# A decoder layer on one core: the two gate rows of the modulation as column sums on VectorE, a DRAM row and a broadcast load, in place of TensorE's sum over partitions

## The chip, the cores and the metric

One core of one Trainium2 chip runs the whole layer in one launch. The metric is the device time in microseconds (us). Before the change it is 745.29 us, the median of 3 runs (744.9 to 745.97).

## The reference, cut to what matters

The kernel computes one decoder layer for T = 512 tokens of width D = 1024: a token-mixing half with two attention branches (16 heads in all, one input projection) and a channel half with a gated MLP of 2 x 2816 hidden columns and a causal convolution of width 3 over the tokens. Each half is scaled, shifted and gated by six rows that come from one conditioning vector c:

```python
mod = c @ w_ada + b_ada
sh1, sc1, gt1, sh2, sc2, gt2 = [m[:, None, :] for m in jnp.split(mod, N_MOD, axis=-1)]
u = x * (1.0 + sc1) + sh1
...
x = _layer_norm(DEEPNORM_ALPHA * x + (1.0 + gt1) * attn_out, ln1_g, ln1_b)
u2 = x * (1.0 + sc2) + sh2
...
x = _layer_norm(DEEPNORM_ALPHA * x + (1.0 + gt2) * ffn_out, ln2_g, ln2_b)
```

The change concerns the two gates, `gt1` and `gt2`, called gate1 and gate2 below, alone. Each is a vector of 1024 numbers that multiplies along the columns of a weight (w_o and w_down), so the kernel needs it as a row repeated on all 128 partitions; shift and scale multiply along the rows of the transposed activations, so they are needed as columns (128 partitions x 8).

## The kernel before, in words

**Stages.** The profile's span falls into these stretches: start, until the first matmul of the input projection at 9.98 us; the first columns of the input projection, k step by k step (L307, to about 50 us); the attention, where heads are interleaved with the rest of the projections (to about 300 us); output projection and first LayerNorm (to about 395 us); the MLP (L1126, 44 steps n, to about 665 us); and the last products with the second LayerNorm (to 743 us). The large matmuls are float32 split into a high and a low part (`wh`, `wl`, made by ScalarE at L183 and VectorE at L93), three products each (L134, L135, L136). The down projection of the MLP is done in a Strassen form, on sums and differences of blocks of w_down, which VectorE makes (L953 to L979).

**Weights.** SyncE issues the loads (L157) in program order into five rotating raw buffers of 128 x 1024; a buffer is loaded again when its last reader is done. For some tiles of w_down, GpSimd issues a second DMA that adds another block onto the loaded tile (L162). The items are taken in one list; the 32 modulation tiles `wa1` are among them.

**Order.** A scheduler with a cost model sets the order of the instructions on TensorE (PE), VectorE (DVE), ScalarE (ACT) and GpSimd (POOL) from the program; only SyncE stays as written. Each engine then runs its list in order, and a wait of one instruction holds all that stand behind it.

**The modulation.** At the start, `mod_sum` (L201) makes shift1 and scale1 as columns: a tile of the transposed w_ada (128 outputs x 1024 inputs) is multiplied on DVE by `cbc`, which is c repeated on all partitions, and summed along the row (`accum_out`). L244 adds 1 to the bias columns of the two scales, and L247 makes the columns `modc` from which ACT makes the first operand `uh` (L273). The later 16 tiles for shift2 and scale2 go the same way (L583).

For the gates, `ada_proc` (L580) takes another layout: four tiles for each half row of 512 outputs, eight blocks of 128 inputs x 512 outputs, which DVE multiplies by a column of c (`cTs`) and adds up (L588 once, L593 seven times). The sum over the 128 partitions is left: `ada_split` (L597) makes the high and low part `ach` and `acl`, and `ada_sum` (L606) multiplies both by a 128 x 128 matrix of ones on PE (L612, L613), so that every partition gets the sum; DVE adds it and 1 (L615) to the bias, which SyncE loaded broadcast over the partitions (L574, 512 KB). There are four half rows: both of gate1 in the attention, the high half of gate2 at n = 10 and 11 of the MLP (L1140, L1142), the low half at n = 28 and 30.

**Who uses them.** gate1 (`gt` of index 0) multiplies the tiles of w_o at L640, from 270.1 us on. gate2 multiplies blocks of w_down: its high half first at L953, at 474.18 us, in a chain L953, L954, L955, L958 and two splits `wdl` (L93) that PE waits for at L1104.

Of the kernel before, what the change touches and what calls it, by code (L numbers as in the profile page):

```python
# [16 lines left out]
P = 128  # L17
T = 512
D = 1024
KT = D // P  # L20
# [28 lines left out]


@with_exitstack
def layer_kernel(ctx: ExitStack, tc: tile.TileContext, out, xT, x, cT, crow, wa0, wa1, bcol, bgt, w1, wct, wv, bf,
                 wp, wo, lncol, lnrow, wup, cwb, wdp):
    nc = tc.nc
    ctx.enter_context(tc.manual_schedule(engines={nc.sync.engine}))
# [3 lines left out]
    t13 = [tc.dram_tile([P, 1024], F32, name=f"t13_{p}") for p in range(FP)]  # L59
    wgt = [tc.dram_tile([P, 512], F32, name=f"wgt_{q}") for q in range(FP)]  # L60
    t24 = tc.dram_tile([P, 1024], F32, name="t24")
    st1 = ExitStack()
    stg = ctx.enter_context(tc.tile_pool(name="stg", bufs=1))
    pp = ctx.enter_context(tc.tile_pool(name="pp", bufs=8, space=PSUM))
# [11 lines left out]
    def bank():  # L76
        return pp.tile([P, 512], F32, name=nm("ps"), tag="ps")
# [5 lines left out]
    def const(shape, dt, s):  # L83
        return cons.tile(shape, dt, name=s, tag=s)
# [4 lines left out]
    def hi_of(o, i, scale=1.0):  # L89
        S.activation(o, i, AF.Copy, scale=scale)  # L90

    def lo_of(o, i, hi):
        state["read"] = V.tensor_tensor(o, i, fl(hi), ALU.subtract)  # L93
        return state["read"]
# [23 lines left out]
    V.tensor_copy(identb, ident)  # L118
    zerob = preset([P, P], BF16, "zerob")
# [8 lines left out]
    modr = const([P, 4, KT, 2], F32, "modr")  # L128

    def z(dt, s, shape=(P, 512)):  # L130
        return zp.tile(list(shape), dt, name=nm(s), tag="z", bufs=NZ)
# [69 lines left out]
    def mod_sum(w, col, wt, c, e):  # L201
        o = modr[:, w, col, e : e + 1]
        state["read"] = V.scalar_tensor_tensor(wt[:, c], wt[:, c], 1.0, cbc[:, c], ALU.mult, ALU.mult, accum_out=o)
        return state["read"]
# [31 lines left out]
    def first_acc(j):  # L236
        wa = pend[j][0]
        if j == 0:
            for e in range(2):
                for q in range(2):  # L240
                    s = mod_sum(q, j, wa[q], slice(e * 512, (e + 1) * 512), e)
            with tc.issue_after(s.ins):
                for q in (1, 3):
                    V.tensor_scalar_add(bcols[:, q, :], bcols[:, q, :], 1.0)  # L244
            for q in range(2):
                raw = modr[:, q, j, :]
                state["modc"] = V.scalar_tensor_tensor(modc[:, q, j : j + 1], raw[:, 0:1], raw[:, 1:2], bcols[:, q, j : j + 1], ALU.add, ALU.add)  # L247
        else:
            mod_col(0, j, wa[0])
            state["modc"] = mod_col(1, j, wa[1])  # L250
# [318 lines left out]
            hi_of(yh[p], yf[p])  # L569
            lo_of(yl[p], yf[p], yh[p])  # L570

    def gt_tile(i):
        t = cons.tile([P, D], F32, name=f"gt{i}", tag="gt")
        nc.sync.dma_start(t, bgt[i : i + 1, :].broadcast_to([P, D]))  # L574
        return t

    gt = [None, None]
    ada_st = {}

    def ada_proc(n):  # L580
        def f(r):
            if 8 <= n < 24:
                mod_sum(2 + (n - 8) // 8, n % 8, r, slice(0, D), 0)  # L583
                return
            g, q = n // 4, n % 4
            if q == 0:
                ada_st[g] = z(F32, "ac2")
                V.tensor_scalar_mul(ada_st[g], r[:, 0:512], cTs[:, 0:1])  # L588
            acc = ada_st[g]
            for e in range(2):  # L590
                k = 2 * q + e
                if k > 0:
                    a = V.scalar_tensor_tensor(acc, r[:, e * 512 : (e + 1) * 512], cTs[:, k : k + 1], acc, ALU.mult, ALU.add)  # L593
                    state["read"] = a
        return f

    def ada_split(g, n):  # L597
        weights(n, 0)
        acc = ada_st[g]
        ah, al = z(F32R, "ach"), z(F32R, "acl")  # L600
        hi_of(ah, acc)
        lo_of(al, acc, ah)
        ada_st[g] = ah, al
        yield 0

    def ada_sum(g):  # L606
        ah, al = ada_st.pop(g)
        ps = bank()
        i = 0 if g < 2 else 1
        if gt[i] is None:  # L610
            gt[i] = gt_tile(i)
        PE.matmul(ps, onesr, ah, start=True, stop=False)  # L612
        PE.matmul(ps, onesr, al, start=False, stop=True)  # L613
# [55 lines left out]
    def add_ada(n=1):  # L669
        for _ in range(n):  # L670
            if skip[0]:
                skip[0] -= 1
            elif adas[0] < 24:
                add_item(wa1[adas[0]], ada_proc(adas[0]))
                adas[0] += 1
                if adas[0] in (4, 8):
                    stream.append((ada_split, (adas[0] // 4 - 1, len(items) - 1)))
                    sums.append([len(stream) + 3, adas[0] // 4 - 1])

    marks = {}  # L680
    seq = PAIRS
# [4 lines left out]

    def flush_sum(n):
        if sums and n >= sums[0][0]:
            stream.append((ada_sum, (sums.pop(0)[1],)))

    wpi = {}

# [612 lines left out]
def _pack(inputs):  # L1305
# [5 lines left out]
    wk = w_ada.reshape(KT, P, 6, D)  # L1311
    r = {}
    r["xT"] = c(a["x"][0].T)
    r["x"] = a["x"][0]
# [7 lines left out]
    r["bcol"] = c(bm[[0, 1, 3, 4]].transpose(2, 0, 1))  # L1322
    r["bgt"] = c(a["b_ada"].reshape(6, D)[[2, 5]])
    def col(kind, n):
        if kind in ("sb", "fox"):
            return (4104 if kind == "sb" else 3080) + n * P
# [23 lines left out]
    return r  # L1350


_NAMES = ["xT", "x", "cT", "crow", "wa0", "wa1", "bcol", "bgt", "w1", "wct", "wv", "bf", "wp", "wo", "lncol", "lnrow",
          "wup", "cwb", "wdp"]


# [17 lines left out]
```

## Time and profile before

| | |
|---|---|
| time, median of 3 runs | 745.29 us (744.9 to 745.97) |
| profiled execution, span | 743.3 us |
| its own time beside the span | the page gives the span alone; the median is 2.0 us above it |
| PE (TensorE matmul) busy | 732.6 us, 99% of the span, 3476 matmuls |
| DVE (VectorE) busy | 607.5 us, 82% |
| ACT (ScalarE) busy | 390.1 us, 52% |
| POOL (GpSimd) busy | 81.5 us, 11% |
| the chain that ended last | PE 98%, POOL 1%, DVE 1% |

A row of the profile names the line of the kernel, the engine, the operation, what is written and read, and how many there were, then the busy time and the mean duration in ns, then the idle time just ahead of them and what ended it. A row of the timeline begins with the start and the duration in us. Matmuls overlap: the duration of one is longer than the distance from its start to the next start, and the distance is what a matmul costs.

### The profile page before, as it was taken

To read this page: it belongs to the slowest core of one execution; us is meant where nothing else is said; L and a number is where in the kernel's file an instruction comes from. 1 tells how busy PE (TensorE), PEld (TensorE's weight loads), DVE (VectorE), ACT (ScalarE), POOL (GpSimd) and SP (SyncE) were. 2 spreads that over 40 slices of the span, in tenths; PEclk is the share of its full clock that TensorE was granted. 3 is DMA by queue.
4 is the path that set the end of the run, shared out by engine and by line. 5 is a ranking of instruction groups with operands and counts; after the bars stand their busy time and mean duration, and the time that the engine had idled before them with its cause. 6 is when DMAs were issued, how large, how long until landed. Compare 5 with 4: busy or idle time off the path is not lost.

```text
span 743.3 us, 9869 instructions
## 1 busy us (share of the span) xinstructions
PE 732.6 (99%) x3476; PEld 608.9 (82%) x3476; DVE 607.5 (82%) x1019; ACT 390.1 (52%) x683; POOL 81.5 (11%) x130
## 2 busy tenths in 40 slices
PE   8999999999999999999999999999999999999995
PEld 5878888888888888888889888888888888888885
DVE  6869789978788795884577889988887797679995
ACT  4567467586876564542055455444454444347550
POOL 1026223335010000000000000000001001000010
PEclk9999999999999999999999999999999999999998
DMA  8944454513422230642052787577788967646633
GB/s 325 405 178 134 151 197 144 171 57 116 170 77 96 101 127 29 228 173 85 1 214 86 227 287 230 196 225 235 253 299 228 253 199 212 212 156 228 230 82 85
DMA packets 45220, 131.95 MB, mean 178 GB/s; under 512 B 5905, under 2 KB 6417, under 8 KB 45170
## 3 DMA queue, kind: packets, MB, share of 16 engines
q1 hardware_dynamic: 38610, 113.66, 44.5%
q0 software_dynamic: 3536, 9.24, 6.4%
q10 hardware_dynamic: 3024, 8.41, 3.1%
q8 instruction: 27, 0.44, 0.2%
q14 instruction: 23, 0.19, 0.1%
HBM read 118.38 MB, written 12.85 MB: 177 GB/s over the span
## 4 chain that ended last, share of the span: by engine, by line
PE 98%; POOL 1%; DVE 1%; DMA 0%; issue 0%; DVEq 0%; POOLq 0%
PE ps L134 19%; PE ps L135 19%; PE ps L136 19%; PE ps L307 5%; PE ps L1103 5%; PE ps L1105 5%; PE ps L1104 5%; PE ps L559 3%; PE ps L541 2%; PE ps L458 2%; PE ps L457 2%; PE ps L459 2%; PE ps L900 2%; PE ps L901 2%; PE ps L902 2%; PE ps L483 1%
## 5 line engine op out<-in xcount | busy, mean ns | idle before, releaser
L183 ACT ACTIVATE wh<-raw 128x1024 fp32r<-128x1024 f32 (+1 forms) x105 | 109.2, 1042 | 109.5 <-PE ps L135 40.4
L93 DVE TENSOR_TENSOR wl<-raw,wh 128x1024 fp32r<-128x1024 f32 (+2 forms) x114 | 135.1, 1187 | 34.6 <-ACT wh L183 33.8
L134 PE MATMUL ps<-u2h,wh 128*128 128x512 f32 (+1 forms) x376 | 141.5, 376 | 0.0
L135 PE MATMUL ps<-u2l,wh 128*128 128x512 f32 (+1 forms) x376 | 141.2, 376 | 0.0
L136 PE MATMUL ps<-u2h,wl 128*128 128x512 f32 (+1 forms) x376 | 141.2, 376 | 0.0
L134 PEld LDWEIGHTS ps<-u2h,wh 128*128 128x128 f32 x376 | 70.8, 188 | 13.4 <-issue 0.6
L136 PEld LDWEIGHTS ps<-u2h,wl 128*128 128x128 f32 x376 | 70.8, 188 | 12.7
L135 PEld LDWEIGHTS ps<-u2l,wh 128*128 128x128 f32 x376 | 70.8, 188 | 12.6
L134 PE MATMUL ps<-uh,wh 128*128 128x512 f32 x200 | 79.5, 398 | 0.0
L135 PE MATMUL ps<-ul,wh 128*128 128x512 f32 x200 | 78.3, 391 | 0.0
L136 PE MATMUL ps<-uh,wl 128*128 128x512 f32 x200 | 78.1, 391 | 0.0
L1153 ACT ACTIVATE cv<-ps,cw 128x512 f32<-128x512 f32 x44 | 34.0, 773 | 42.4 <-PE ps L136 36.4
L1154 DVE SCALAR_TENSOR_TENSOR cv<-ps,cw,cv 128x511 f32<-128x511 f32 x44 | 32.8, 745 | 17.0 <-ACT cv L1153 17.0
L136 PEld LDWEIGHTS ps<-uh,wl 128*128 128x128 f32 x200 | 37.6, 188 | 8.2
L134 PEld LDWEIGHTS ps<-uh,wh 128*128 128x128 f32 x200 | 37.6, 188 | 7.3
L135 PEld LDWEIGHTS ps<-ul,wh 128*128 128x128 f32 x200 | 37.7, 188 | 7.1
L521 POOL TENSOR_TENSOR pt<-pt,om 128x127 f32<-128x127 f32 (+3 forms) x32 | 41.6, 1312 | 7.7 <-DVE om L520 7.7
L162 POOL DMA_DIRECT2D raw<-in_wdp x10 | 9.4, 942 | 249.2 <-DVE cv L1155 183.9
L1155 DVE SCALAR_TENSOR_TENSOR cv<-ps,cw,cv 128x510 f32<-128x510 f32 x44 | 32.7, 744 | 0.3
L1161 ACT ACTIVATE cv<-cv 128x512 f32<-128x512 f32 x22 | 13.9, 630 | 34.4 <-DVE cv L1155 34.4
L520 DVE TENSOR_TENSOR_SCAN om<-om,dg 128x127 f32<-128x127 f32 (+3 forms) x32 | 28.5, 946 | 0.1
L1105 PE MATMUL ps<-wh,hv 128*128 128x512 f32 x72 | 28.0, 389 | 0.0
(235 smaller groups left out, 1582.9 us busy)
## 6 DMA issues: line engine op xcount, KB each, us to landing
raw<-in_wup SPq DMA_DIRECT2D x44, 512.0 KB, 5.4
raw<-in_wa SPq DMA_DIRECT2D x32, 512.0 KB, 4.2
raw<-in_wct SPq DMA_DIRECT2D x25, 512.0 KB, 3.7
raw<-in_wdp SPq DMA_DIRECT2D x20, 512.0 KB, 5.4
wa<-in_wa SPq DMA_DIRECT2D x14, 512.0 KB, 8.1
raw<-in_wdp SPq DMA_DIRECT2D x22, 256.0 KB, 4.3
raw<-t SPq DMA_DIRECT2D x22, 256.0 KB, 3.8
raw<-in_wdp POOLq DMA_DIRECT2D x10, 512.0 KB, 7.7
```

Of the source, the lines that this page charges most:

```text
L93: state["read"] = V.tensor_tensor(o, i, fl(hi), ALU.subtract)
L134: PE.matmul(ps, wh, ah, start=first, stop=False)
L135: PE.matmul(ps, wh, al, start=False, stop=False)
L136: return PE.matmul(ps, wl, ah, start=False, stop=last)
L183: state["hi"] = S.activation(h[:, 0:cols], r[:, 0:cols], AF.Copy)
L307: PE.matmul(grp[g], w, u, start=j == 0 and n == 0, stop=j == KT - 1 and n == (1 if g == 7 else 2))
L521: G.tensor_tensor(pt[b][:, s : e - 1], pt[b][:, s : e - 1], om[:, s + 1 : e], ALU.mult)
L1103: PE.matmul(ps, ah, bh, start=first, stop=False, skip_group_check=onto)
L1104: PE.matmul(ps, ah, bl, start=False, stop=False, skip_group_check=onto)
L1105: return PE.matmul(ps, al, bh, start=False, stop=last, skip_group_check=onto)
L1153: S.activation(t, ps, AF.Identity, bias=cw[:, n, 3:4], scale=cw[:, n, 2:3])
L1154: V.scalar_tensor_tensor(t[:, 1:], ps[:, 0:511], cw[:, n, 1:2], t[:, 1:], ALU.mult, ALU.add)
```

## The change

All six rows now come as columns. `wa1` holds the transposed w_ada for the gates as well, in 16 further tiles that `mod_sum` takes (16 DVE operations over 128 x 1024 in place of 4 + 28 over 128 x 512). A new function `gate_rows` then adds the bias columns on DVE (`gcol`), stores them from GpSimd's queue to a row in DRAM (`grow`, element by element, since a column of 128 partitions becomes 128 neighbours in the row), and loads that row, broadcast, into `gt`, also from GpSimd's queue, behind a wait for the store. It is called once for gate1 (1024 numbers) and twice for gate2 (512 numbers each, at n = 11 and 30). Gone are `ada_split`, `ada_sum` with its 8 matmuls, the matrix of ones `onesr` and its copy at the start, and the two broadcast loads of the bias. L244 adds 1 to four rows of bias columns, not two. `cbc` is now read until the last gate tile.

```diff
-    bcols = const([P, 4, KT], F32, "bcols")
+    bcols = const([P, 6, KT], F32, "bcols")
...
-    onesr = const([P, P], F32R, "onesr")
-    V.tensor_copy(onesr, ones)
...
-                for q in (1, 3):
+                for q in (1, 3, 4, 5):
                     V.tensor_scalar_add(bcols[:, q, :], bcols[:, q, :], 1.0)
...
     def ada_proc(n):
         def f(r):
-            if 8 <= n < 24:
-                mod_sum(2 + (n - 8) // 8, n % 8, r, slice(0, D), 0)
-                return
-            g, q = n // 4, n % 4
-            if q == 0:
-                ada_st[g] = z(F32, "ac2")
-                V.tensor_scalar_mul(ada_st[g], r[:, 0:512], cTs[:, 0:1])
-            acc = ada_st[g]
-            for e in range(2):
-                k = 2 * q + e
-                if k > 0:
-                    a = V.scalar_tensor_tensor(acc, r[:, e * 512 : (e + 1) * 512], cTs[:, k : k + 1], acc, ALU.mult, ALU.add)
-                    state["read"] = a
+            mod_sum((4, 2, 3, 5)[n // 8], n % 8, r, slice(0, D), 0)
         return f
...
-        ah, al = z(F32R, "ach"), z(F32R, "acl")
-        hi_of(ah, acc)
-        lo_of(al, acc, ah)
...
-        PE.matmul(ps, onesr, ah, start=True, stop=False)
-        PE.matmul(ps, onesr, al, start=False, stop=True)
-        t = gt[i][:, (g % 2) * 512 : (g % 2 + 1) * 512]
-        V.scalar_tensor_tensor(t, ps, 1.0, t, ALU.add, ALU.add)
-        yield 4
+    def gate_rows(i, j0, j1):
+        if gt[i] is None:
+            gt[i] = cons.tile([P, D], F32, name=f"gt{i}", tag="gt")
+        c, d = slice(j0 * P, j1 * P), gcol[:, i, j0:j1]
+        V.tensor_tensor(d, modr[:, 4 + i, j0:j1, 0], bcols[:, 4 + i, j0:j1], ALU.add)
+        G.dma_start(grow[i][:, c].rearrange("o (j p) -> (o p) j", p=P), d)
+        G.dma_start(gt[i][:, c], grow[i][:, c].broadcast_to([P, (j1 - j0) * P]))
+        yield 0
...
             if n in (10, 28):
-                list(ada_split(7 if n == 10 else 6, wai[n]))
+                weights(wai[n], 0)
             if n in (11, 30):
-                list(ada_sum(7 if n == 11 else 6))
+                list(gate_rows(1, *((4, 8) if n == 11 else (0, 4))))
...
-    kf = wk[:, :, [2, 5]].reshape(4, 2, P, 2, 2, 512).transpose(3, 4, 0, 2, 1, 5).reshape(2, 8, P, D)
-    r["wa1"] = c(np.concatenate([kf[0], wt[3], wt[4], kf[1]], axis=0))
+    r["wa1"] = c(wt[2:6].reshape(32, P, D))
```

The scheduler places the new instructions among the old ones. In the rows below, the number at the end of a name is that of the buffer, and the changed kernel's own line numbers stand (its L94 is L93 of before, L910 and L911 are L936 and L937, L927 to L932 are L953 to L958, L954 is L980, L1128 and L1129 are L1154 and L1155).

On DVE at the start, before: the four sums of the first modulation tiles, the two additions of 1, the two columns `modc`, and the cast of a small matrix.

```order
L203 SCALAR_TENSOR_TENSOR wa_158,modr<-wa_158,cbc 128x512 [waits DMAHW5_49]
L244 TENSOR_SCALAR bcols<-bcols 128x8 [waits DMAHW0_49]
L244 TENSOR_SCALAR bcols<-bcols 128x8
L247 SCALAR_TENSOR_TENSOR modc<-modr,bcols 128x1 [waits DVE_49] x2
L118 CAST identb<-ident 128x128 [waits Pool_49]
L284 TENSOR_SCALAR xt_160<-xt_160,modc 128x512 [waits DMAHW7_49,Activation_49]
```

The same place in the changed kernel:

```order
L203 SCALAR_TENSOR_TENSOR wa_159,modr<-wa_159,cbc 128x512 [waits DMAHW5_49]
L244 TENSOR_SCALAR bcols<-bcols 128x8 [waits DMAHW0_49]
L244 TENSOR_SCALAR bcols<-bcols 128x8 x3
L247 SCALAR_TENSOR_TENSOR modc<-modr,bcols 128x1 [waits DVE_49]
L117 CAST identb<-ident 128x128 [waits Pool_49]
L247 SCALAR_TENSOR_TENSOR modc<-modr,bcols 128x1 [waits DVE_49]
```

Two more additions stand ahead of the columns, and the cast has moved in between them, ahead of the second column.

On POOL in the first third of the MLP, before: the last small transfers of the attention, the three accumulating DMAs onto tiles of w_down, and the store of a block that DVE made.

```order
L379 DMA s_3_551<-chi 2x1x512
L380 DMA m_3_555<-chi 2x1x512
L162 DMA raw_4083<-in_wdp 128x1024
L162 DMA raw_4323<-in_wdp 128x1024
L162 DMA raw_4485<-in_wdp 128x1024
L980 DMA wgt_73<-rs_4670 128x512
```

The same place in the changed kernel, from the second accumulating DMA on, with what each waits for:

```order
L162 DMA raw_4297<-in_wdp 128x1024 [waits DMAHW4_49,DMAHW1_49,DMAHW5_49,DMAHW0_49,DMAHW7_49,DMASW3_49,DVE_49]
L162 DMA raw_4455<-in_wdp 128x1024 [waits DMAHW1_49,DMAHW3_49,DMASW4_49,DVE_49]
L588 DMA grow_86<-gcol 128x4x1 [waits DMASW5_49,DVE_49]
L589 DMA gt_4505<-grow_86 128x512 [waits DMASW6_49,DMASW5_49]
L954 DMA wgt_73<-rs_4636 128x512 [waits DMASW7_49,DVE_49]
```

The store and the load of the high half of gate2 stand behind the third accumulating DMA; the load waits for the store.

On DVE in the same stretch, where `gcol` stands in the changed kernel (in the kernel before, L615 stands 20 rows later):

```order
L94 TENSOR_TENSOR wl_4460<-raw_4453,wh_4459 128x1024
L1129 SCALAR_TENSOR_TENSOR cv_4448<-ps_4407,cw,cv_4448 128x510
L587 TENSOR_TENSOR gcol<-modr,bcols 128x4
L910 TENSOR_TENSOR xn_3489<-xn_3489,lnr_4210 128x512
L910 TENSOR_TENSOR xn_3588<-xn_3588,lnr_4209 128x512
```

Further down DVE's list, before, the chain that reads the gate:

```order
L93 TENSOR_TENSOR fo_4593<-cv_4478,fh_4592 128x256
L953 TENSOR_TENSOR wg_4607<-raw_4601,gt_4538 128x512
L937 TENSOR_TENSOR xn_3726<-xn_3726,lnr_4241 128x512
L954 TENSOR_TENSOR raw_4601<-raw_4601,raw_4485 128x512
L955 TENSOR_TENSOR raw_4601<-raw_4601 128x512
L958 TENSOR_TENSOR raw_4485<-raw_4485,gt_4538 128x512
L93 TENSOR_TENSOR wdl_4613<-raw_4601,wdh_4611 128x512
L93 TENSOR_TENSOR wdl_4614<-raw_4601,wdh_4612 128x512
```

and in the changed kernel, with what it waits for:

```order
L94 TENSOR_TENSOR fo_4559<-cv_4448,fh_4558 128x256 [waits Activation_49]
L927 TENSOR_TENSOR wg_4573<-raw_4567,gt_4505 128x512 [waits DMAHW4_49,DMASW6_49]
L928 TENSOR_TENSOR raw_4567<-raw_4567,raw_4455 128x512 [waits DMASW4_49,DVE_49]
L929 TENSOR_TENSOR raw_4567<-raw_4567 128x512 [waits DVE_49]
L932 TENSOR_TENSOR raw_4455<-raw_4455,gt_4505 128x512
```

The chain keeps its place behind the last `fo`; it waits for a DMA of GpSimd's queue (DMASW6, the load of `gt`), and the row of LayerNorm work that stood within it has moved ahead.

More of the change, by code (lines that the diff above doesn't have):

```diff
@@ L51, in layer_kernel @@
 @with_exitstack
-def layer_kernel(ctx: ExitStack, tc: tile.TileContext, out, xT, x, cT, crow, wa0, wa1, bcol, bgt, w1, wct, wv, bf,
+def layer_kernel(ctx: ExitStack, tc: tile.TileContext, out, xT, x, cT, crow, wa0, wa1, bcol, w1, wct, wv, bf,
                  wp, wo, lncol, lnrow, wup, cwb, wdp):
@@ L61, in layer_kernel @@
     t24 = tc.dram_tile([P, 1024], F32, name="t24")
+    grow = [tc.dram_tile([1, D], F32, name=f"grow{i}") for i in range(2)]
     st1 = ExitStack()
@@ L127, in layer_kernel @@
     modc = const([P, 4, KT], F32, "modc")
-    modr = const([P, 4, KT, 2], F32, "modr")
+    modr = const([P, 6, KT, 2], F32, "modr")
+    gcol = const([P, 2, KT], F32, "gcol")
     def z(dt, s, shape=(P, 512)):
@@ L570, in stage_c, with ada_done @@
             lo_of(yl[p], yf[p], yh[p])
[L572 to L575, printed above, removed]
     gt = [None, None]
[L578 removed]
     def ada_proc(n):
         def f(r):
[L582 to L594 removed]
+            mod_sum((4, 2, 3, 5)[n // 8], n % 8, r, slice(0, D), 0)
         return f
[L597 removed]
+    def ada_done(n):
         weights(n, 0)
[L599 to L603 removed]
         yield 0
[L606 to L609, printed above, removed]
+    def gate_rows(i, j0, j1):
         if gt[i] is None:
[L611 to L616 removed]
+            gt[i] = cons.tile([P, D], F32, name=f"gt{i}", tag="gt")
[4 more added lines that the diff above has]
+        yield 0
     sg, ma, wps = {}, {}, {}
@@ L675, in add_ada @@
                 adas[0] += 1
-                if adas[0] in (4, 8):
-                    stream.append((ada_split, (adas[0] // 4 - 1, len(items) - 1)))
-                    sums.append([len(stream) + 3, adas[0] // 4 - 1])
+                if adas[0] == 8:
+                    stream.append((ada_done, (len(items) - 1,)))
+                    sums.append([len(stream) + 3, (0, 0, KT)])
     marks = {}
@@ L688, in flush_sum @@
         if sums and n >= sums[0][0]:
-            stream.append((ada_sum, (sums.pop(0)[1],)))
+            stream.append((gate_rows, sums.pop(0)[1]))
     wpi = {}
@@ L1310, in _pack @@
     w_in, w_ada = a["w_in"], a["w_ada"]
-    wk = w_ada.reshape(KT, P, 6, D)
     r = {}
@@ L1318, in _pack @@
     r["wa0"] = c(wt[0:2].transpose(1, 0, 2, 3))
[L1319 to L1320 removed]
+    r["wa1"] = c(wt[2:6].reshape(32, P, D))
     bm = a["b_ada"].reshape(6, KT, P)
[L1322 to L1323 removed]
+    r["bcol"] = c(bm[[0, 1, 3, 4, 2, 5]].transpose(2, 0, 1))
     def col(kind, n):
@@ L1350, in _pack @@
     return r
-_NAMES = ["xT", "x", "cT", "crow", "wa0", "wa1", "bcol", "bgt", "w1", "wct", "wv", "bf", "wp", "wo", "lncol", "lnrow",
+_NAMES = ["xT", "x", "cT", "crow", "wa0", "wa1", "bcol", "w1", "wct", "wv", "bf", "wp", "wo", "lncol", "lnrow",
           "wup", "cwb", "wdp"]
```

## The prediction

> **What bounds the kernel now.** I read the page's busy times first, then its chain, then the waits of TensorE (PE), then PE's timeline at the places that the change touches. The page's first part, and from its fourth the shares of the chain that ended last:
>
> ```profile
> span 743.3 us, 9869 instructions
> PE 732.6 (99%) x3476; PEld 608.9 (82%) x3476; DVE 607.5 (82%) x1019; ACT 390.1 (52%) x683; POOL 81.5 (11%) x130
> PE 98%; POOL 1%; DVE 1%; DMA 0%; issue 0%; DVEq 0%; POOLq 0%
> ```
>
> PE's waits, all that the trace has:
>
> ```profile
> PE ps L196 <- DMA cbr<-in_crow: 2.4, 1, 2.4
> PE ps L483 <- POOL m L349: 0.2, 1, 0.2
> ```
>
> PE waits once before the start and once for 0.2 us. So from its first projection matmul on, it has a list of matmuls and runs it without a gap. A matmul taken off the list is worth its distance to the next start; work taken off the other engines is worth nothing while nobody on PE waits for it; and a new wait costs what exceeds its slack, once, because PE cannot catch up later. The span is 743.3 us and the median 745.29 us; the 2.0 us between them lie around the span (or between executions), and I take them as unchanged. All differences below are worked out on the span and applied to the median.
>
> **Removed from PE.** The eight matmuls over the matrix of ones, as groups:
>
> ```profile
> L613 PE MATMUL ps<-acl,onesr 128*128 128x512 f32 x4 | 1.6, 394 | 0.0
> L612 PE MATMUL ps<-ach,onesr 128*128 128x512 f32 x4 | 1.6, 392 | 0.0
> ```
>
> Their durations overlap with their neighbours', so the price is read from the starts on PE's timeline, for the pair of the high half of gate2:
>
> ```profile
> 462.73 0.39 PE L612 MATMUL ps<-ach,onesr 128*128 128x512 f32 x1
> 462.96 0.40 PE L613 MATMUL ps<-acl,onesr 128*128 128x512 f32 x1
> 463.19 0.41 PE L134 MATMUL ps<-u2h,wh 128*128 128x512 f32 x1
> ```
>
> From 462.73 to 463.19 are 0.46 us for two: 0.23 each, 8 x 0.23 = 1.8 us off the span. The durations would have given 1.6 + 1.6 = 3.2 us, nearly twice that.
>
> **Removed from and added to the other engines.** DVE loses its accumulation (and four each of three smaller steps), and gains 16 sums over a whole tile, as shift2 and scale2 have them:
>
> ```profile
> L593 DVE SCALAR_TENSOR_TENSOR ac<-raw,cTs,ac 128x512 f32<-128x512 f32 x28 | 23.1, 826 | 0.4
> L203 DVE SCALAR_TENSOR_TENSOR raw<-raw,cbc 128x1024 f32<-128x1024 f32 x16 | 20.4, 1273 | 1.4 <-DMA raw<-in_wa 1.3
> ```
>
> The 28 steps were 23.1 us, and 16 more of the last row come to 20.4: DVE has a few us less to do. None of it counts, since PE waits for DVE nowhere; for the same reason ACT's four `ach` and the two 512 KB loads of the bias are worth nothing. Four places can cost: the start, the attention, and the two halves of gate2.
>
> **The start.** DVE now has two more additions and one cast ahead of the second column of `modc`, and ACT's first operand waits for that column. DVE, ACT, PE at the start:
>
> ```profile
> 8.31 0.24 DVE L244 TENSOR_SCALAR bcols<-bcols 128x8 f32<-128x8 f32 x2
> 8.46 0.34 DVE L247 SCALAR_TENSOR_TENSOR modc<-modr,bcols 128x1 f32<-128x1 f32 x2
> 8.71 0.22 DVE L118 CAST identb<-ident 128x128 bf16<-128x128 f32 x1
> ...
> 8.94 0.81 ACT L273 ACTIVATE uh<-xt,modc 128x512 fp32r<-128x512 f32 x1 [0.23 <-DVE identb L118]
> ...
> 9.98 1.68 PE L307 MATMUL ps<-uh,wh 128*128 128x512 f32 x5
> ```
>
> Two additions took 0.15 us from start to start (8.31 to 8.46), the cast at most 0.22. If the column is what ACT waits for, `uh` and with it PE comes 0.15 to 0.35 us later; if it is the landing of `xt`, which the row doesn't show, part of it is hidden. I take 0.2 us, bounds 0 and 0.35. Nothing gives it back: PE has no gap behind it.
>
> **The attention.** The store and load of gate1 stand on POOL between two heads' multiplications. POOL's idle time there, and the first reader of gate1 in the list of what reads `gt`:
>
> ```profile
> 106.79 0.10 POOL L517 MEMSET pt<- 128x2 f32 x1 [13.88 <-ACT pt L516]
> ...
> L640 DVE TENSOR_TENSOR raw<-raw,gt x8: 1211/1220/1226, 270.1 to 331.1; 128x1024 f32<-128x1024 f32 x8
> ```
>
> A store and a load of some 3 to 5 us each (rows below) fit into 13.9 us, unless `gcol` comes at the end of that stretch; then the multiplications behind are late by up to one transfer, some 5 us, against which their results have the time that PE spends on other items between heads. Price 0, bounds 0 and 5. Gate1 itself has until 270.1.
>
> **The high half of gate2, the place that decides.** On POOL the store and the load stand behind the third accumulating DMA, and DVE's chain for the first block of w_down stands behind the load. The timeline of POOL and of DVE, and the first matmuls that use the chain's result:
>
> ```profile
> 456.51 1.15 POOL L162 DMA_DIRECT2D raw<-in_wdp  x1 [20.45 <-DMA raw<-in_wdp]
> ...
> 458.81 0.74 DVE L1155 SCALAR_TENSOR_TENSOR cv<-ps,cw,cv 128x510 f32<-128x510 f32 x1
> ...
> 474.18 0.68 DVE L953 TENSOR_TENSOR wg<-raw,gt 128x512 f32<-128x512 f32 x1
> 474.79 0.68 DVE L937 TENSOR_TENSOR xn<-xn,lnr 128x512 f32<-128x512 f32 x1
> ...
> 477.31 1.29 DVE L93 TENSOR_TENSOR wdl<-raw,wdh 128x512 fp32r<-128x512 f32 x2
> ...
> L1104 PE MATMUL ps<-wdl,fh x2: 389/389/389, 479.8 to 480.5; 128*128 128x512 f32 x2
> ```
>
> In the changed order `gcol` follows the L1155 of 458.81, so it is done at about 459.6. Before, the chain from 474.18 ends with the first `wdl` at about 478.0, and PE takes it at 479.8: slack 1.8 us. In the changed order the row of L937 (0.6) has left the chain, so it takes 3.2 us, and PE is 6 matmuls earlier by then (6 x 0.23 = 1.4): the chain must start by 479.8 - 1.4 - 3.2 = 475.2 on the clock of before. The load must have landed by then; from 459.6 that is 15.6 us for issue and flight of both DMAs. Rows of landings, in the DMA issues:
>
> ```profile
> lnr<-in_lnrow SPq DMA_DIRECT2D x4, 256.0 KB, 5.1
> s<-chi POOLq DMA_DIRECT2D x8, 4.0 KB, 1.7
> DMA to landing us min/median/max: 5.6/7.1/9.7
> ```
>
> No row shows a store of 512 pieces of 4 bytes. Its bounds are the small store from POOL's queue (1.7) and the slowest of the accumulating DMAs L162 (9.7, the last row, which is L162's own); I take 3.5 us, nearer the small one, since it carries 2 KB, and more, since its pieces are many. The load is 128 rows of 2 KB out of one DRAM row, as the broadcast `lnr` (5.1); the bounds are 2.6 (taken as half of 5.1) and 9.7. With 0.5 for the handover on POOL (a guess) it lands at 459.6 + 3.5 + 0.5 + 5.1 = 468.7, 6.5 us ahead. At both upper ends it lands at 459.6 + 9.7 + 9.7 = 479.0, 3.8 us late. So I take 0, bounds 0 and 3.8. DVE has no idle time in which a wait would vanish, by the busy times of this window (PE, PEld, DVE, ACT, POOL; then the granted clock, 1.00):
>
> ```profile
> 456.00:478.60 22.60, 22.60 (x101) 18.48 (x100) 22.57 (x37) 7.32 (x12) 1.15 (x1) 1.00 0.59 188
> ```
>
> 22.57 of 22.60 us busy. Behind L953 on DVE stand the splits and the convolution (L1154, L1155) of the following steps; PE would wait for `wdl` first.
>
> How far the issue itself can go under such a DVE, L162 shows:
>
> ```profile
> L162 POOL DMA_DIRECT2D raw<-in_wdp x10: 857/884/1222, 406.7 to 631.1; - x10
> ```
>
> The issue at 456.51 took 1.15 us against a median of 0.88, for a tile of 128 rows. If POOL's time went with the number of pieces, the store's 512 would take 4 x 1.15 = 4.6 us to issue, and the load would land at 459.6 + 4.6 + 3.5 + 1.15 + 5.1 = 474.0, still 1.2 us ahead.
>
> A rule of the Trainium skill speaks against the change here ("SBUF — State Buffer", A bandwidth-pool intuition that's wrong): DVE can lock a port that GpSimd needs for a DMA of its own queue, and one of 620 ns then takes 3100 ns. By it the two DMAs would take 5 us more than alone. So far the trace speaks against it: the L162 beside a DVE without a gap took 0.3 us over the median, not 2.5. It is rival (d) below. That a strided last dimension becomes one descriptor per element ("DMA: Bandwidth & Descriptors", Rules for kernel authors) is not shown by any row here.
>
> **The low half of gate2** is issued at n = 30, in the stretch ahead of 560 us, where POOL does nothing:
>
> ```profile
> 559.97 0.57 POOL L980 DMA_DIRECT2D t<-rs  x1 [24.25 <-DVE rs L979]
> ...
> L1185 DVE TENSOR_TENSOR tm<-u,gt x2: 680/680/680, 684.2 to 686.0; 128x512 f32<-128x512 f32 x2
> ```
>
> POOL is idle for 24.25 us ahead of 559.97, and L1185 is the first reader of that half. Price 0; were POOL not idle, the store of `t` would be what comes late. On SyncE's queue the two loads of the second LayerNorm's rows now wait for the last gate sum (`cbc` shares their memory), and hold the weight loads behind them. PE waits for no such load in the whole trace; I take 0, bound 1.
>
> **Sum.** -1.8 + 0.2 + 0 + 0 + 0 = -1.6 us: 745.29 - 1.6 = 743.7 us, 0.2% less. About 0.2% (1.5 us) is also what a measurement of this kernel can tell from no change: the bounds are 743.8 and 746.8, so the forecast lies at the edge of faster.
>
> **Rivals.** (a) *The gate lands late.* The two DMAs in sequence take over 15.6 us: pieces that POOL writes one by one, behind DVE's work, with landings as slow as L162's worst. DVE stands at L953 with everything behind it, and PE waits at L1104. It decides from a landing of 475.2 on, and makes the kernel slower than before when the wait exceeds the 1.6 us saved; at the upper bounds 3.8 us, 745.29 - 1.6 + 3.8 = 747.5. For it: 4.6 us of issue and one landing of 9.7 in place of 5.1 already give 478.6, 3.4 us late. Against: 6.5 us to spare at the nearest rows. (b) *The gain is eaten in small pieces.* The full 0.35 us at the start (743.8), with SyncE's late load or another wait of up to 1 us: 743.8 to 744.9, within the bounds of no change. For it: PE has no slack at 9.98. Against: each single term is small. (c) *POOL is blocked in the attention* with a gate1 store that waits for `gcol` past 106.79: a head comes up to 5 us late, 743.7 to 748.7. For it: 1024 pieces in that store. Against: 13.9 us of idle POOL. (d) *POOL's issues are held by DVE*: if each of the two waited for four of DVE's operations of 0.68 us, they would be 2 x 2.7 = 5.4 us later than the slow estimate of 474.0, so the load lands at 479.4, 4.2 us late: 745.29 - 1.6 + 4.2 = 747.9. For it: DVE without a gap. Against: the 1.15 us of the L162. The page on SBUF named above would have it so. That the change doesn't do what it says is out: the eight matmuls are gone from PE's list.
>
> **Chances.** Forecast 0.62 (743.2 to 744.2, of which I count 0.5 as faster and 0.12 as same), (a) 0.13 (0.08 slower, 0.05 within the bounds), (b) 0.15 (all same), (c) 0.06 (0.04 slower, 0.02 same), (d) 0.04 (slower). Faster 0.50, same 0.12 + 0.05 + 0.15 + 0.02 = 0.34, slower 0.08 + 0.04 + 0.04 = 0.16. The range holds the forecast with the spread of the runs (0.4 us below it), (b), and about half of (a) and (c): 742.8 to 747.0.
>
> **What would show it.** Right: PE's matmul count 8 lower, PE's waits as before, the first L307 at about 10.2, L927 (the old L953) on DVE with no idle time ahead of it, the load of `gt` issued by about 464 and landed by 470. Wrong: a PE wait at L1104's line for `wdl`, idle DVE ahead of L927 on a DMA `gt`, a store of `gcol` of over 8 us, or a first L307 later than 10.4; and a span shorter by more than 2.5 us would mean that PE lost time which its timeline does not show as a wait.

## The result, and the profile after

The changed kernel takes 755.68 us, the median of 5 runs (755.33 to 760.12), against 745.86 us (744.9 to 745.97) for the kernel before in as many runs: a ratio of 1.0157, with a 95% interval of 1.0137 to 1.0177. It is slower by 9.8 us, where 743.7 us and a range of 742.8 to 747.0 were forecast. The profiled execution took 758.94 us, 3.3 us over the median, so the sizes below are that execution's and their sum is larger than the median's loss.

The page of the changed kernel: span, busy times, and the chain that ended last by engine.

```profile
span 757.2 us, 9836 instructions
PE 735.2 (97%) x3468; PEld 609.6 (81%) x3468; DVE 599.1 (79%) x1015; ACT 387.7 (51%) x679; POOL 82.5 (11%) x136
PE 82%; DMA 6%; DVE 5%; issue 3%; ACT 1%; POOL 1%; SPq 0%; ACTq 0%; DVEq 0%; POOLq 0%
```

The eight matmuls are gone (3468 of 3476), and yet TensorE (PE) is busy 2.6 us longer: part of its matmuls ran at a lower clock. The chain now has DMA and VectorE (DVE) in it. All that PE waited for:

```profile
PE ps L134 <- DVE cv L1129: 3.8, 1, 3.8
PE ps L196 <- DMA cbr<-in_crow: 2.4, 1, 2.4
PE ps L1077 <- ACT hv L91: 1.6, 1, 1.6
PE ps L483 <- DVE m L94: 1.3, 1, 1.3
PE ps L559 <- DVE vv L94: 1.3, 1, 1.3
PE ps L482 <- DVE pl L94: 1.3, 1, 1.3
PE ps L541 <- DVE vv L94: 1.3, 1, 1.3
PE ps L483 <- POOL m L349: 0.2, 1, 0.2
```

Five of the eight are new waits for DVE, one for ScalarE (ACT). To see where they lie, I took the same matmul in the timelines of both kernels and subtracted its starts. How far the changed kernel lags behind the one before, by the time in the kernel before:

| stretch (us, kernel before) | lag at its start | lag at its end | what happens in it |
|---|---|---|---|
| 15 to 85 | 0.4 | 0.3 | start and first heads |
| 85 to 100 | 0.3 | 3.3 | PE waits for `vv` (L541, L559) |
| 112 to 125 | 3.5 | 8.5 | PE waits for `m`, `pl` (L482, L483), behind the first store |
| 125 to 400 | 8.5 | 6.8 | four of the removed matmuls, and a list in another order |
| 455 to 470 | 6.8 | 6.3 | two of the removed matmuls |
| 478 to 500 | 6.3 | 8.3 | the high half of gate2 lands late |
| 575 to 583 | 8.3 | 13.8 | PE waits at L134, behind the third store |
| 583 to 730 | 13.8 | 13.5 | two of the removed matmuls |

**The store lands late.** The landings of the three stores, in the source view of L588:

```profile
L588 POOL DMA_DIRECT2D grow<-gcol x3: 784/794/1107, 102.8 to 552.3; - x3
DMA to landing us min/median/max: 12.8/13.8/14.4
```

The issue on GpSimd (POOL) takes 0.8 to 1.1 us; the landing comes after 12.8 to 14.4 us, where 3.5 was taken and 9.7 was the upper bound. The load that follows lands in 4.0 to 5.8, near the 5.1 taken. So DVE waits for the high half of gate2, in DVE's timeline:

```profile
482.93 0.69 DVE L927 TENSOR_TENSOR wg<-raw,gt 128x512 f32<-128x512 f32 x1 [3.63 <-DMA gt<-grow]
```

**And it slows everything else.** The windows around the first store (issued at 102.79) in the changed kernel; the columns are the length, PE, PEld, DVE, ACT and POOL with counts, the granted clock, the DMA engines' share and GB/s:

```profile
102.00:107.00 5.00, 5.00 (x26) 4.27 (x25) 3.58 (x7) 2.32 (x5) 1.11 (x1) 1.00 0.90 266
107.00:117.00 10.00, 10.00 (x52) 8.42 (x51) 2.41 (x4) 7.02 (x14) 0.00 (x0) 1.00 0.88 69
110.00:130.00 20.00, 17.34 (x77) 13.91 (x77) 9.40 (x13) 7.91 (x14) 5.00 (x10) 0.91 0.57 133
```

and the same 10 us in the kernel before:

```profile
107.00:117.00 10.00, 10.00 (x53) 8.50 (x52) 9.89 (x12) 7.93 (x15) 5.19 (x6) 1.00 0.59 215
```

The DMA engines are 88% busy from 107 to 117 us and move 69 GB/s; before, they moved 215 GB/s at 59%. DVE does 2.41 us of work in place of 9.89. Two of its waits for weight tiles, in DVE's timeline:

```profile
90.85 1.22 DVE L203 SCALAR_TENSOR_TENSOR raw<-raw,cbc 128x1024 f32<-128x1024 f32 x1 [3.75 <-DMA raw<-in_wa]
119.16 1.26 DVE L203 SCALAR_TENSOR_TENSOR raw<-raw,cbc 128x1024 f32<-128x1024 f32 x1 [9.33 <-DMA raw<-in_wa]
```

and of the second wait, the load in the chain (start and duration in us):

```profile
104.07 14.64 DMA raw<-in_wa
```

A weight tile issued 1.3 us behind the store takes 14.64 us to land, against a median of 4.2 for such tiles before. PE works on until 121 us, waits for `m` and then for `pl`, and when it starts again its clock is lower (0.91 in the mean of 110 to 130): its matmuls stand 0.43 us apart at 127 us, not 0.23. The wait at 90.85 comes ahead of the first store, though. It is another thing: a column sum (L203) stands in DVE's list ahead of the `vv` that PE needs, and its tile has not landed. In the kernel before, the `vv` of that place come first, from 86.27 to 97.33 us, and the next sums of gate1 behind them:

```profile
86.27 0.42 DVE L93 TENSOR_TENSOR vv<-ps,vv 128x256 fp32r<-128x256 f32 x1
...
99.05 2.33 DVE L593 SCALAR_TENSOR_TENSOR ac<-raw,cTs,ac 128x512 f32<-128x512 f32 x3
```

Behind the third store (issued at 552.26, landed at 566.05) the price is paid late. Two windows of the changed kernel, and a load in its chain:

```profile
557.00:566.00 9.00, 9.00 (x41) 7.47 (x40) 8.93 (x16) 5.62 (x12) 0.00 (x0) 1.00 1.03 136
576.00:586.00 10.00, 9.95 (x44) 7.89 (x43) 4.02 (x7) 1.92 (x3) 0.85 (x1) 1.00 1.03 299
576.35 9.21 DMA raw<-in_wup
```

The transfers that the other queues issued from 551.60 to 554.68 take 15.0 to 15.7 us. What has piled up keeps the DMA engines full until 586: a load issued 10 us after the store has landed still takes 9.21 us, and PE's wait of 3.8 us at L134 ends at 589.78.

### The profile page after: what moved, and what is told of

Its sections match the earlier page's. It is cut to its first block, busy times and chain, and to the rows that moved or that the text cites. A ratio compares the mean times of both kernels' runs of the same rounds, so it can differ in the third digit from the quotient of the medians.

```text
span 757.2 us, 9836 instructions
## 1 busy us (share of the span) xinstructions
PE 735.2 (97%) x3468; PEld 609.6 (81%) x3468; DVE 599.1 (79%) x1015; ACT 387.7 (51%) x679; POOL 82.5 (11%) x136
## 3 DMA queue, kind: packets, MB, share of 16 engines
HBM read 118.39 MB, written 12.85 MB: 173 GB/s over the span
## 4 chain that ended last, share of the span: by engine, by line
PE 82%; DMA 6%; DVE 5%; issue 3%; ACT 1%; POOL 1%; SPq 0%; ACTq 0%; DVEq 0%; POOLq 0%
PE ps L134 16%; PE ps L135 16%; PE ps L136 16%; PE ps L307 5%; PE ps L1077 5%; PE ps L1079 4%; PE ps L1078 4%; DMA raw<-in_wa 3%; PE ps L559 2%; PE ps L876 2%; PE ps L874 2%; PE ps L875 2%; PE ps L541 2%; DVE wl L94 1%; PE ps L482 1%
## 5 line engine op out<-in xcount | busy, mean ns | idle before, releaser
L94 DVE TENSOR_TENSOR wl<-raw,wh 128x1024 fp32r<-128x1024 f32 (+2 forms) x114 | 135.5, 1190 | 31.7 <-ACT wh L183 31.4
L134 PE MATMUL ps<-u2h,wh 128*128 128x512 f32 (+1 forms) x376 | 141.8, 378 | 3.8 <-DVE cv L1129 3.8
L134 PEld LDWEIGHTS ps<-u2h,wh 128*128 128x128 f32 x376 | 70.9, 189 | 17.1 <-issue 4.2
L134 PE MATMUL ps<-uh,wh 128*128 128x512 f32 x200 | 80.0, 400 | 0.0
L203 DVE SCALAR_TENSOR_TENSOR raw<-raw,cbc 128x1024 f32<-128x1024 f32 x32 | 39.3, 1230 | 24.8 <-DMA raw<-in_wa 24.8
L1128 DVE SCALAR_TENSOR_TENSOR cv<-ps,cw,cv 128x511 f32<-128x511 f32 x44 | 32.8, 745 | 21.9 <-ACT cv L1127 21.9
L134 PEld LDWEIGHTS ps<-uh,wh 128*128 128x128 f32 x200 | 38.0, 190 | 7.3
L521 POOL TENSOR_TENSOR pt<-pt,om 128x127 f32<-128x127 f32 (+3 forms) x32 | 39.0, 1234 | 12.1 <-DVE om L520 12.0
L1129 DVE SCALAR_TENSOR_TENSOR cv<-ps,cw,cv 128x510 f32<-128x510 f32 x44 | 32.7, 743 | 0.4
```

The lines of the kernel that those rows point to most:

```text
L134: PE.matmul(ps, wh, ah, start=first, stop=False)
L521: G.tensor_tensor(pt[b][:, s : e - 1], pt[b][:, s : e - 1], om[:, s + 1 : e], ALU.mult)
L1128: V.scalar_tensor_tensor(t[:, 1:], ps[:, 0:511], cw[:, n, 1:2], t[:, 1:], ALU.mult, ALU.add)
L1129: V.scalar_tensor_tensor(t[:, 2:], ps[:, 0:510], cw[:, n, 0:1], t[:, 2:], ALU.mult, ALU.add)
```

## The experiments

Theory S says that the stores of 4-byte pieces, which land late and hold up all other DMA traffic, are most of the loss. The rivals are P (the 16 column sums stand too early in DVE's list) and Q (a DMA from GpSimd's queue is what is slow, whatever it carries). All ratios are to the kernel before on the same chip, with 95% intervals.

**e1: no store.**

```diff
-        G.dma_start(grow[i][:, c].rearrange("o (j p) -> (o p) j", p=P), d)
-        G.dma_start(gt[i][:, c], grow[i][:, c].broadcast_to([P, (j1 - j0) * P]))
+        G.dma_start(gt[i][:, c], lnrow[i : i + 1, c].broadcast_to([P, (j1 - j0) * P]))
```

> The changed kernel without the store; the load into gt fetches a row of the LayerNorm's parameters instead of the stored one, so the gates' values are left out of the result. Theory S (the store of 4-byte pieces lands after 13 to 14 us and slows all other DMA traffic meanwhile, and that is most of the loss): the waits at 102 to 125, at 478 and at 576 to 590 us go, and 745 to 748 us are left. Rival P (the 16 column sums stand too early in DVE's list and make it wait for their tiles, whatever the store does): over 752 us. Between the two, 748 to 752, both count.

748.13 us (745.62 to 749.86), ratio 1.0028 (1.0013 to 1.0042). The loss falls from 9.8 us to 2.6. But this run does more than leave out the store: the loads now read an input, so the scheduler was free to move them, and it put the first at the start, ahead of the load of the activations `xt` (rows of POOL and of the chain):

```profile
3.23 0.73 POOL L588 DMA_DIRECT2D gt<-in_lnrow  x1
3.44 6.79 DMA xt<-in_xT
```

In the changed kernel `xt` takes 5.76 us there. The profiled execution of e1 lags by 2.9 us at the start, probably for this reason; from 85 to 100 us it loses 3.3 us more, as the changed kernel does, and nothing at 112 to 125 or 575 to 583. The cleaner test is e2, whose instructions stand in the changed kernel's order on all engines.

**e2: the store in 128 contiguous pieces.**

```diff
-        G.dma_start(grow[i][:, c].rearrange("o (j p) -> (o p) j", p=P), d)
+        G.dma_start(grow[i][:, c].rearrange("o (p j) -> (o p) j", p=P), d)
```

> The changed kernel with a store of 128 contiguous pieces of 32 or 16 bytes in place of 1024 or 512 pieces of 4 bytes; same queue, same load, but the row then holds the gates in another order, so the result is permuted. Theory S by the number of pieces: the store lands after 2 to 5 us, the GB/s behind it stay over 150, and the time is that of the kernel without a store within 1.5 us. Rival Q (a small store from GpSimd's queue is slow of itself, by its handover): it lands after over 10 us as before, and the time stays over 753 us. Rival P: over 752 us with a quick store.

745.85 us (745.23 to 748.32), ratio 1.0006 (0.9994 to 1.0017). The source view of L588:

```profile
DMA to landing us min/median/max: 5.0/5.8/6.4
```

and the window behind the first store (issued at 102.31):

```profile
107.00:117.00 10.00, 10.00 (x53) 8.48 (x52) 9.12 (x13) 8.14 (x16) 5.07 (x8) 1.00 0.35 126
```

The store lands in 5.0 to 6.4 us, and DVE works 9.12 of 10 us. The 126 GB/s are below the 150 expected, but at a share of 0.35: there is less to move, and nothing is held up. Q falls: same queue, same bytes, same order of instructions.

**e3: the store added to the kernel before.**

```diff
         V.scalar_tensor_tensor(t, ps, 1.0, t, ALU.add, ALU.add)
+        if g != 0:
+            j0, j1 = {1: (0, 8), 7: (4, 8), 6: (0, 4)}[g]
+            G.dma_start(grow[i][:, j0 * P : j1 * P].rearrange("o (j p) -> (o p) j", p=P), bcols[:, 1, j0:j1])
```

> The kernel before, with three stores of 4-byte pieces added on GpSimd's queue at the places of the gates (1024, 512 and 512 pieces of a column tile that is there anyway); nobody reads them. Theory S: each store slows the loads for some 8 us, and the kernel gets slower than before by 2 to 8 us, 747 to 753. Rival P: no effect, 745.3 to 746.3.

754.48 us (753.46 to 756.62), ratio 1.0118 (1.0093 to 1.0143). It is not what was planned: what it stores is ready at the start, so the scheduler put all three stores there, and the loss lies there too.

```profile
8.40 1.10 POOL L619 DMA_DIRECT2D grow<-bcols  x1 [5.11 <-DVE modc L248]
...
9.53 1.55 POOL L619 DMA_DIRECT2D grow<-bcols  x2
```

which are POOL's rows of the start, and among PE's waits stands

```profile
PE ps L308 <- ACT uh L274: 7.3, 1, 7.3
```

Where the first weights are loaded, three stores that nobody reads make PE wait 7.3 us, and the lag is 9.5 us with the slower clock behind it. From 12 to 20 us the DMA engines are full in both kernels (shares of 1.10 and 1.03), but move 139 GB/s here and 409 in the kernel before, and loads issued from 6.82 to 9.06 us take 17.1 to 17.9 us to land (7.5 to 8.7 before). That the stores hold up loads is shown; what they cost at the gates' places was left to e8.

**e4: the store from ACT's queue.**

```diff
-        G.dma_start(grow[i][:, c].rearrange("o (j p) -> (o p) j", p=P), d)
+        S.dma_start(grow[i][:, c].rearrange("o (j p) -> (o p) j", p=P), d)
```

> The changed kernel with the store issued from ScalarE's queue; the load stays with GpSimd. Theory S: the store lands as late (over 10 us) and slows the other traffic as much, 752 to 760 us. Rival Q (GpSimd's own descriptors are what is slow): the store lands in under 5 us, 745 to 750 us.

755.79 us (753.54 to 758.45), ratio 1.0133 (1.0102 to 1.0165). The view of L588:

```profile
L588 ACTq DMA_DIRECT2D grow<-gcol x3: 377/377/427, 103.6 to 554.5; - x3
DMA to landing us min/median/max: 11.6/11.6/11.6
```

Issued in 0.38 us by another engine, it lands as late: one landing is on record, 11.6 us, and the loads that wait for the three stores are issued 12.1 to 13.7 us behind them. Q falls a second time, and with it rival (d) of the prediction: GpSimd's issue has no part in the lateness of the store.

**e8: the store added, in its place.** As e3, but it reads the finished `gt`, so it cannot be moved ahead.

```diff
+        if g != 0:
+            w = 8 if g == 1 else 4
+            G.dma_start(grow[i][:, 0 : w * P].rearrange("o (j p) -> (o p) j", p=P), t[:, 0:w])
```

> The kernel before with three stores of 4-byte pieces that read the finished gt tile, so that they stand where the gates are made and not at the start; nobody reads what they store. Theory S: each slows the loads for 8 to 12 us, at about 117, 465 and 586 us, and the kernel is 3 to 10 us slower than before, 748.5 to 755.5. Rival (only the gate's own lateness and the sums' placement cost in the changed kernel): 745 to 746.5.

760.54 us (759.93 to 760.95), ratio 1.0192 (1.0176 to 1.0208): 15 us, more than expected. PE's two longest waits behind the stores:

```profile
PE ps L560 <- DVE m L94: 6.5, 1, 6.5
PE ps L135 <- DVE cv L1159: 4.7, 1, 4.7
```

and the windows behind the first store (issued at 145.1):

```profile
148.00:156.00 8.00, 8.00 (x44) 6.84 (x43) 0.86 (x2) 7.11 (x14) 0.62 (x2) 1.00 0.92 32
156.00:166.00 10.00, 3.52 (x15) 2.63 (x14) 7.15 (x9) 6.04 (x9) 4.76 (x6) 0.77 0.06 9
```

32 GB/s at a share of 0.92, then PE busy for 3.52 of 10 us, at a clock of 0.77. By the lag of the same matmuls, the first store costs 8.0 us, the second nothing, the third 7.6. No instruction waits for these stores, so beside the 0.8 to 1.1 us of POOL for each issue, which e10 has too, they can cost only by what they do to other transfers. That one of three costs nothing fits a price that depends on the slack of the loads in flight behind it; no run measures that slack.

**e9 and e10: is it the number of pieces, or that they are neighbours?** Both have e8's order of instructions on all engines.

```diff
-            G.dma_start(grow[i][:, 0 : w * P].rearrange("o (j p) -> (o p) j", p=P), t[:, 0:w])
+            G.dma_start(grow[i][:, 0:P].rearrange("o (j p) -> (o p) j", p=P), t[:, 0:1])                  # e9
+            G.dma_start(grow[i][0 : w * P, 0:1].rearrange("(j p) o -> p (j o)", p=P), t[:, 0:w])   # e10, grow[i] is [D, 16]
```

> As e8_store_in_place (the kernel before with three stores that nobody reads), but each store has 128 pieces of 4 bytes, neighbours in the row, in place of 1024, 512 and 512. If the number of pieces is what costs: landings of 2 to 5 us and a time of 745 to 747 us. If a store of 4-byte pieces costs the same however many there are: landings of 8 to 12 us and over 752 us.

> As e8_store_in_place, with 1024, 512 and 512 pieces of 4 bytes that lie 64 bytes apart in DRAM and not side by side. If neighbouring pieces stand in each other's way in DRAM: landings of 3 to 6 us and under 749 us. If the number of pieces alone costs: landings of 8 to 12 us and over 755 us, as e8_store_in_place.

e9: 756.87 us (754.15 to 758.43), ratio 1.0147 (1.0123 to 1.0172). e10: 745.29 us (744.5 to 747.04), ratio 1.0000 (0.9991 to 1.0010). The source view of the store in e9:

```profile
L619 POOL DMA_DIRECT2D grow<-gt x3: 570/574/748, 143.9 to 592.2; - x3
DMA to landing us min/median/max: 7.9/8.9/9.8
```

and in e10:

```profile
L619 POOL DMA_DIRECT2D grow<-gt x3: 790/794/1104, 144.3 to 586.1; - x3
DMA to landing us min/median/max: 2.2/3.1/3.6
```

with the window that in e8 moved 32 GB/s:

```profile
148.00:156.00 8.00, 8.00 (x44) 6.81 (x43) 7.02 (x10) 7.15 (x15) 5.34 (x8) 1.00 0.07 24
```

Three stores of 128 pieces side by side, 512 bytes each, cost 11.5 us; 1024, 512 and 512 pieces of the same 4 bytes, 64 bytes apart, cost nothing and land in 2.2 to 3.6 us. In e10 the share behind the store is 0.07: the loads had landed by then, and DVE worked on them. The weight tile issued 0.9 us behind the first store took 12.85 us in e8 and 4.41 in e10. It is the neighbourhood in DRAM that costs; the number of pieces alone does not.

**e5: the whole change, with contiguous pieces.** As e2, with the gates' rows of w_ada and their bias laid out so that partition p holds neighbouring outputs; the row then comes in its order.

```diff
-    r["wa1"] = c(wt[2:6].reshape(32, P, D))
+    def rows(m, w):
+        g1 = m[2].reshape(P, KT, w).swapaxes(0, 1)
+        g2 = m[5].reshape(2, P, 4, w).swapaxes(1, 2).reshape(KT, P, w)
+        return g1, g2
+    g1, g2 = rows(w_ada.T.reshape(6, D, D), D)
+    r["wa1"] = c(np.concatenate([g1, wt[3], wt[4], g2], axis=0))
...
```

> The whole change with contiguous pieces: the rows of w_ada and the bias columns of the gates are laid out so that partition p holds neighbouring outputs, and the store of 128 pieces of 32 or 16 bytes gives the row in its right order. By the sum so far: 1.8 us less for the eight matmuls, 2 to 3 us more for the column sums that stand too early in DVE's list at 85 to 100 us (theory P', what the runs without the element store left over), so 745.2 to 747 us. Rival (what was left over is chance or the start): 743.5 to 744.5.

747.11 us (745.91 to 748.33), ratio 1.0019 (1.0010 to 1.0028), above the kernel before although eight matmuls are gone. What is left over is PE's wait for `vv`, in PE's waits and in DVE's timeline:

```profile
PE ps L541 <- DVE vv L94: 2.0, 1, 2.0
PE ps L559 <- DVE vv L94: 1.3, 1, 1.3
```

```profile
91.26 1.23 DVE L203 SCALAR_TENSOR_TENSOR raw<-raw,cbc 128x1024 f32<-128x1024 f32 x1 [3.26 <-DMA raw<-in_wa]
...
92.41 0.42 DVE L94 TENSOR_TENSOR vv<-ps,vv 128x256 fp32r<-128x256 f32 x1
```

**e6: as e5, three gate tiles later in the list of weights.** (`skip` leaves out the next tiles of the modulation; they follow at the end.)

```diff
     marks["v1"] = len(stream)
+    skip[0] = 3
```

> As e5_rows_valid, with three of the gate tiles put later in the list of weights, so that in DVE's list no column sum stands between the evacuations of the values at 86 to 98 us. Theory P': the waits of TensorE at L541 and L559 for vv go, and the time is 743.2 to 744.7 us. Rival (the loss of the attention has another cause): as e5_rows_valid within 0.5 us, 745 or more.

743.91 us (743.01 to 744.66), ratio 0.9972 (0.9961 to 0.9984): faster than both. All of PE's waits:

```profile
PE ps L196 <- DMA cbr<-in_crow: 2.4, 1, 2.4
PE ps L1078 <- DVE cv L1130: 0.6, 1, 0.6
PE ps L559 <- DVE vv L94: 0.3, 1, 0.3
PE ps L483 <- POOL m L349: 0.2, 1, 0.2
```

The same stretch in DVE's timeline:

```profile
85.22 1.23 DVE L203 SCALAR_TENSOR_TENSOR raw<-raw,cbc 128x1024 f32<-128x1024 f32 x1 [4.38 <-DMA raw<-in_wa]
...
87.50 0.42 DVE L94 TENSOR_TENSOR vv<-ps,vv 128x256 fp32r<-128x256 f32 x1
```

DVE still waits for the tiles of the column sums, 10.5 us in the whole kernel (16.7 in e5), and 4.38 us just here; but no sum stands between the `vv` any more. The time is about that of the forecast for the change itself.

**e7: gate2 alone.** The kernel before with e5's way for gate2, while gate1 stays with PE:

```diff
+            if n >= 24:
+                mod_sum(4, n % 8, r, slice(0, D), 0)
+                return
...
-                list(ada_sum(7 if n == 11 else 6))
+                list(gate_rows(1, *((4, 8) if n == 11 else (0, 4))))
```

> The kernel before with gate2 alone changed, by column sums and contiguous stores; gate1 stays with TensorE. Four matmuls fewer and nothing moved in the attention: 745.5 - 0.9 = 744.6, 744.2 to 745.2 us. Rival (the load of the high half is late even with a store of 5 to 6 us): a wait at the first product of the down projection, over 745.5.

745.25 us (744.27 to 746.15), ratio 0.9992 (0.9983 to 1.0001). Inconclusive: the sign is as expected, the size is not. In its profile the lag is -0.8 us from 500 to 575, and two waits of 0.6 and 0.5 us for DVE's `cv` give it back.

**e11: the changed kernel, store and all, with e6's `skip`.**

> The changed kernel with the store of 4-byte pieces, and three of the gate tiles later in the list of weights as in e6_rows_later. Theory: store and placement of the sums add up, so the waits for vv go and those behind the stores stay: 2 to 4 us less than the changed kernel, 751.5 to 754 us, unless the first store meets other loads. Rival (the store is all): 755 us or more.

748.97 us, but between 743.88 and 752.51 over 10 runs; ratio 1.0042 (1.0017 to 1.0067). It is faster than expected. Its stores land as late:

```profile
L588 POOL DMA_DIRECT2D grow<-gcol x3: 784/794/1104, 120.8 to 546.5; - x3
DMA to landing us min/median/max: 11.7/12.3/12.5
```

but the first, issued at 120.8 and not at 102.8, costs nothing in the profiled execution; the second and the third cost 4.6 us and 3.7 us. Little else is on its way beside that first store (the last load ahead of it lands at 121.84 us, the next is issued at 128.68), and it still takes 11.7 us: it is slow of itself, and not because of the transfers beside it. So the two causes do not add up: by the medians the move is worth 755.68 - 748.97 = 6.7 us with the store, and 747.11 - 743.91 = 3.2 without it. The spread of 9 us from run to run fits a cost that hangs on which loads are on their way; that is argued, not tested.

## Why the prediction was wrong

**The gain was right.** The lag falls by 0.5 us for each pair of removed matmuls (455 to 470, 583 to 600), and e6 shows 743.91 us where 743.7 was the sum without a stall. That these two agree so closely is in part luck, since PE still waits for DVE for 0.9 us in e6 (0.6 and 0.3).

**The price of the store was wrong, and so was its kind.** The prediction bounded the store by the nearest rows, 1.7 and 9.7 us, and took 3.5; it landed in 12.8 to 14.4. The bounds came from stores and loads with whole rows of 2 KB or more, and none of them writes 4-byte neighbours. This alone makes rival (a): the gate is late at L927 by 3.63 us, and costs 2.0 us on PE. Two of the prediction's own signs of being wrong came true with it, idle DVE ahead of L927 and a store of over 8 us. But the larger error is that the store was priced only by who waits for it. What it did to the other transfers had no term: the weight loads behind it cost 5.0 us in the attention (112 to 125) and 5.5 us in the MLP (575 to 583). The low half of gate2 was put at 0 because POOL is idle there and its reader is far; both are so, and that store is the dearest one in the profiled execution. e8 shows it clean: three stores that nobody reads cost 15 us. So of the terms that the sum has at 0, the profiled execution shows 8.0 us in the attention (5.0 of them from the store), 2.0 at the high half and 5.5 at the low half.

Rival (c), POOL blocked in the attention, came true in POOL's timeline, by the late landing and not by a late `gcol`: POOL stands for 13.56 us until 117.46, with the next multiplications behind the load of gate1. But the chain that ended last goes through the weight load and DVE there, and not through POOL, and in e8 no POOL instruction waits for the store.

**"None of it counts, since PE waits for DVE nowhere" was wrong for a reason of its own.** DVE has less to do, as said (599.1 us, 607.5 before), but the order changed. Before, the sums of gate1's later tiles stood behind the evacuations of the values; as single column sums they stand between them, ahead of `vv`, and wait for tiles in flight (3.75 us at 90.85). PE then waits twice for 1.3 us: 3.0 us of lag from 85 to 100. The prediction read the order around the gate2 chain and at the start, and not where the sums of gate1 had moved. e5 against e6 shows this term at 3.2 us.

**The start** was put at 0.2 us with bounds of 0 and 0.35. The first L307 starts at 9.98 us before, at 10.16 in the changed kernel, and at 9.99 and 9.75 in e5 and e6, which have the same two additions. No run tells it from 0.

**Rival (d) and a nearer rule.** By the rule on GpSimd's port that the prediction cites for rival (d), the kernel would have been slower, as it was, but for another cause: the store's issue took 0.8 to 1.1 us, and from ACT's queue the store was as late (e4). The Trainium skill has a nearer one ("DMA: Bandwidth & Descriptors", Specifications): below 512 bytes a DMA engine does a read-modify-write. By itself that does not tell e8 from e10, whose pieces are of the same 4 bytes.

What stays open: how much of the profiled execution's 5.5 us at 575 to 583 is in the median run, which is 3.3 us shorter; why neighbours hold up the other queues' transfers (the runs show that they do); and from which size or distance of the pieces on they do not, between 4 and 16 bytes and between 4 and 64 bytes apart.

## What to carry to other kernels

A DMA has two prices: when its own reader gets it, and what it does to the transfers beside it; where weights stream in with a few us of slack, ask the second question of every small store. A column of 128 partitions goes to a DRAM row in contiguous pieces per partition, with the order of the outputs arranged in the weights' layout, not as 4-byte neighbours. When work is cut into new instructions, read in the new order what now stands behind each of them and whether what it waits for has landed: an engine with spare time can still stand in the way.

## What the runs showed of the hardware

Stores of 4-byte pieces from 128 partitions that are neighbours in DRAM land in 7.9 to 9.8 us for 128 pieces (e9), 8.5 and 12.1 for 512 and 1024 (e8), and 12.8 to 14.4 in the changed kernel; with hardly any other transfer on its way, one still took 11.7 (e11). The same pieces 64 bytes apart land in 2.2 to 3.6 (e10), and neighbouring pieces of 16 or 32 bytes in 1.9 to 8.0 (e2 and e5 to e7), the longest of them while the queues moved 346 GB/s. While neighbours of 4 bytes are written, the other queues' loads come to a crawl: 69 GB/s at a share of 0.88 in the changed kernel, 139 in place of 409 GB/s at a full share in e3, and a weight tile that takes 12.85 us in place of 4.41 (e8, e10). 512 bytes written this way, three times, cost a kernel of 745 us 1.5% (e9).

A wait of PE of some us cost more than itself: PE waited 6.5 us behind the first store of e8, the granted clock was 0.77 from 156 to 166 us, and the lag was 8.0 us; after its waits the changed kernel's matmuls stood 0.43 us apart at 127 us.
